# Five small constants move to the far end of SBUF, so that pools begin at multiples of 512 bytes

## The chip, the core and the metric

The kernel runs on one core of a Trainium2 chip. The core has a matrix engine (PE, with its weight loads shown apart as PEld), a vector engine (DVE), a scalar engine (ACT), GpSimd (POOL) and a sync engine (SP) that here only issues transfers. Operands live in SBUF, 128 partitions of on-chip memory; an address in this document is a byte offset within a partition, the same in all 128. Matmul results go to PSUM. The metric is the device time of one execution in microseconds, as the median of several runs. Lower is better.

## The reference

The reference is one layer of a hybrid decoder block on a sequence of 1024 tokens of width 1024, followed by a final RMS norm.

```python
mod = jax.nn.silu(c) @ ada_w + ada_b
shift, scale, gate = jnp.split(mod, 3, axis=-1)
h = rms_norm(x, norm_w) * (1 + scale[:, None, :]) + shift[:, None, :]
proj = h @ w_in
gm_u, gm_v, gm_z, ssm_z, xbc, dt_raw, g_a, g_b = jnp.split(proj, SPLITS, axis=-1)
y_a = spatial_gating(gelu(gm_u), gelu(gm_v), ...) * silu(gm_z)
xbc = silu(causal_depthwise_conv(xbc, conv_w, conv_b))
y_b = ssd_scan(xh, dt, a, bmat, cmat) + xh * d_skip[:, None]
y_b = rms_norm(y_b * silu(ssm_z), ssm_norm_w)          # per group
merged = sigmoid(g_a) * (y_a @ w_proj_a) + sigmoid(g_b) * (y_b @ w_proj_b)
x = x + gate[:, None, :] * (merged @ w_out)
out = rms_norm(x, final_norm_w)
```

By far the largest product is `h @ w_in` (1024 x 1024 by 1024 x 11296). The other large ones are `y_a @ w_proj_a`, `y_b @ w_proj_b` (inner width 2048) and `merged @ w_out`.

## The kernel before

All matrices are fp32. A large product is done in three passes of a one-pass fp32 format ("fp32r"): each operand is split into a high part and a low remainder, and high x high, high x low and low x high are accumulated. So most matmuls have the same shape: a stationary block of 128 x 128 and a moving block of 128 x 512, both fp32r, that is 512 bytes and 2048 bytes per partition. `w_in`, `w_proj_b` and `w_out` also go through a Strassen-like scheme with seven products named p1 to p7, whose sums DVE forms.

The stages in order of time:

- **Stage 1.** The input is loaded, normalised and transposed; the rows of h are made (`rows_of_h`) and split into 56 tiles of 2048 bytes in `hpool`. The first columns of the projection are multiplied beside this (`first_products`, through the helper `mm`, line 76, with stationary pieces `w0h` and `w0l` from the pool `p0`).
- **The pair stage.** `pair` works through the column blocks of `w_in`, two at a time; `product` issues its matmuls in line 560. The moving operands are the split tiles in `hpool`, the stationary operands are split weights in `wpool`. This takes more than half of the kernel. Results go through DVE and ACT into `wide` tiles in `w4pool`.
- **The SSD stage.** The scan over chunks, in fp32, with `y_a @ w_proj_a` (`proj_a`, tile `pma`, line 76) drawn in between to keep PE busy. All operands of `proj_a` are in `hpool`. The scan's tiles are in `p2r`, `p2q` and `p2x`.
- **The product with `w_proj_b`.** `multiply`, line 1459: seven products of 8 units, each unit 12 matmuls. The moving operands (`p1bh`, `p1bl` and so on) are in `hpool`; the stationary operands (`p1a` and so on, from the helper `big`) are in `p2r` and `p2q`.
- **The product with `w_out`.** `out_products`, line 1658. Its operands come from whatever has room: `hpool`, `p2r`, `p2q`.
- **The end.** The last norm factors and the stores.

The order on PE is written out by hand and pinned. DVE and ACT are ordered by a planner. Transfers are issued from SP and ACT; a buffer that is used again makes its next load wait for the last reader.

SBUF is given out by pools from both ends. A pool on the left starts where the pool below it ended; a pool on the right ends where the one above it began. Pools that are closed give their bytes to later pools, and a tile then waits for the last users of every tile whose bytes it overlaps. A tile starts at a multiple of 32 bytes. The first pool, `const`, begins at byte 16512; the usable memory ends at byte 229344. This gives the following starts before the change, worked out by the allocator from the sizes:

| pool | side | starts at | start modulo 512 | holds |
|---|---|---|---|---|
| const | left | 16512 | 128 | identity, masks, parameters |
| hpool | left | 24448 | 384 | split rows of h, later ring buffers and operands |
| p0 | left | 139136 | 384 | stage 1 |
| wpool, wspool | left | 139136, 171904 | 384, 384 | weights of the pair stage |
| w4pool | right | 204768 | 480 | `wide` tiles |
| gmpool, gxpool | right | 198624, 192832 | 480, 320 | mixer |
| prepool | right | 189408 | 480 | preparation of `w_proj_b` |
| p2r | right | 188384 | 480 | SSD, weights of line 1459 and 1658 |
| p2x, p2q | right | 172000, 139232 | 480, 480 | SSD, later operands |

Nearly every large tile is a multiple of 512 bytes long, so it has its pool's start modulo 512. The stationary operands of stage 1 are windows into tiles of 1152 bytes and start at 0, 128, 256 or 384 modulo 512.

The helpers that record most matmuls and transfers:

```python
def mm(acc, l, r, first=True, last=True):
    pin(PE.matmul(acc, l, r, start=first, stop=last))
...
def load(dst, src):
    pin(nc.sync.dma_start(dst, src))
```

The rest that the change touches is the block of constants near the start of the kernel. Of these, `sc` is read by the modulation and the gate of stage 1, `dtb` and `abc` by the step sizes (`dt_part1a`, `dt_part1d`), `dsk` and `dskt` by `small_parameters` and by `evacuate` (a per-partition factor).

Of the kernel before, what the change touches and what calls it, by code (L numbers as in the profile page):

```python
# [8 lines left out]
F32 = mybir.dt.float32  # L9
# [7 lines left out]
P = 128  # L17
D = 1024
S = 1024
KT = D // P  # L20
NCH = S // P
NG = 8
HPG = 4
NH = 32
# [11 lines left out]
def hybrid_kernel(  # L36
# [33 lines left out]
    def cst(shape, name, dt=F32):  # L70
        return const.tile(shape, dt, name=name, tag=name)

    pin = tc.keep_in_program_order

    def mm(acc, l, r, first=True, last=True):
# [33 lines left out]
    par = cst([P, P], "par")  # L109
    par2 = cst([P, P], "par2")  # L110
    cwt = cst([P, P], "cwt")
    dtb = cst([P, NH], "dtb")
    abc = cst([P, NH], "abc")
    dskt = cst([P, 16], "dskt")
    dsk = cst([P, NH], "dsk")
    sc = cst([P, KT], "sc")
    dthq = cst([P, NCH * NH], "dthq")
    dde = cst([P, NCH * NH], "dde")
    nacs = cst([P, NCH * NH], "nacs")
    cd = cst([P, NCH * NH], "cd")  # L120
    ssq = cst([P, NG * NCH], "ssq")
    conv_wt = cwt.rearrange("p (k i) -> p k i", k=4)
    conv_bt = par2[:, 0:32]
    snw = par2[:, 32:48]
# [1670 lines left out]
```

## Time and profile before

| | |
|---|---|
| median of 3 runs | 1415.43 us (1413.42 to 1416.88) |
| span of the profiled execution, first to last instruction | 1412.0 us |
| PE busy | 1386.7 us, 98% of the span, 7051 matmuls |
| PE weight loads | 1147.0 us, 81% |
| DVE, ACT, POOL busy | 1062.5, 796.2, 212.5 us |
| DMA | 283.13 MB, 201 GB/s over the span |
| mean granted PE clock | 0.998 |

The profile is one execution. No other time is listed for it than its span; the median of the runs is 3.4 us above that, which is start and end work outside the span. A row of the timeline gives start, length, engine, line, operation, tiles, shapes and count. The length of a matmul's record is longer than its share of PE, because matmuls overlap: the pace of PE is the distance from one start to the next. In the table of windows each row has the stretch, its length, then for each engine the busy time and the count, the granted clock, the DMA share and GB/s.

### The profile page before, as it was taken

What the parts mean: (1) busy time and instruction counts of PE and PEld (TensorE: products, weight loads), DVE (VectorE), ACT (ScalarE), POOL (GpSimd) and SP (SyncE); (2) the same over time, 40 slices, a digit from 0 to 9 for tenths busy, and PEclk for the clock granted to TensorE, in tenths of its full rate; (3) what the DMA queues carried; (4) which work ended last, traced back from release to release, by engine and by line L of the source; (5) the groups of instructions that cost most, each with busy time, mean ns of one, the idle gap of its engine ahead of it and who ended that gap; (6) DMA issues with size and microseconds to landing.
All of it is one profiled execution on the core that took longest, in us unless ns stands there. A gap on an engine that the chain in (4) does not pass through costs nothing. (4 is left out here: it accounts for less than half of the span.)

```text
span 1412.0 us, 20661 instructions
## 1 busy us (share of the span) xinstructions
PE 1386.7 (98%) x7051; PEld 1147.0 (81%) x7051; DVE 1062.5 (75%) x1863; ACT 796.2 (56%) x1471; POOL 212.5 (15%) x208
## 2 busy tenths in 40 slices
PE   8999999999999999999999999999999999999997
PEld 7788888888888888887888888888888878777886
DVE  5686677767778899788888785388777767866866
ACT  6664575656656665555666555586766723322443
POOL 0000000000000011110100010027878830000001
PEclk9999999999999999999999999999999999999999
DMA  8552333343344667777675774498878759867903
GB/s 269 159 166 83 127 104 108 102 128 110 121 135 127 199 197 236 244 239 233 203 205 175 243 213 134 167 347 313 279 268 286 275 188 347 307 219 267 374 6 120
DMA packets 271918, 283.13 MB, mean 201 GB/s; under 512 B 14300, under 2 KB 222596, under 8 KB 271812
## 3 DMA queue, kind: packets, MB, share of 16 engines
q1 hardware_dynamic: 184548, 198.39, 44.0%
q10 hardware_dynamic: 87264, 83.41, 17.7%
q8 instruction: 56, 0.92, 0.3%
q14 instruction: 50, 0.41, 0.1%
HBM read 194.42 MB, written 87.33 MB: 200 GB/s over the span
## 5 line engine op out<-in xcount | busy, mean ns | idle before, releaser
L775 POOL TENSOR_TENSOR wog<-wog,gb 128x256 f32<-128x256 f32 x16 | 17.0, 1080 | 673.5 <-DMA wog<-in_w_out_dram 673.5
L989 ACT ACTIVATE dcy<-dcy,nacs 128x128 f32<-128x128 f32 x256 | 78.6, 389 | 15.2 <-POOL dcy L984 14.8
L984 POOL TENSOR_SCALAR_AFFINE_SELECT dcy<-dcy 128x1024 f32<-128x1024 f32 x32 | 35.0, 1094 | 138.2 <-ACT ea L981 134.6
L902 ACT ACTIVATE ac<-ac 128x1024 f32<-128x1024 f32 x32 | 33.9, 1060 | 25.9 <-DVE ac L900 25.8
L981 ACT ACTIVATE ea<-dcy 64x512 f32<-64x512 f32 x64 | 40.1, 626 | 14.7 <-DMA dcy<-acs_d 14.2
L76 PE MATMUL pma<-yh,wah 128*128 128x512 f32 x128 | 43.3, 419 | 0.0
L76 PE MATMUL pma<-yh,wal 128*128 128x512 f32 x128 | 42.6, 414 | 0.0
L1071 POOL TENSOR_TENSOR yz<-y,sl 128x512 f32<-128x512 f32 x32 | 41.5, 1296 | 1.1
L1009 DVE TENSOR_TENSOR dcy<-dcy,pc 128x1024 f32<-128x1024 f32 x32 | 38.9, 1216 | 2.9 <-PE pc L79 1.4
L1069 DVE TENSOR_TENSOR ym<-yn,ea 128x512 f32<-128x512 f32 (+1 forms) x32 | 19.9, 622 | 27.3 <-PE yn L76 27.3
L76 PE MATMUL pma<-yl,wah 128*128 128x512 f32 x128 | 40.2, 395 | 0.0
L1070 POOL TENSOR_TENSOR y<-y,ym 128x512 f32<-128x512 f32 (+1 forms) x32 | 36.6, 1143 | 12.0 <-DVE ym L1069 11.2
L76 PEld LDWEIGHTS yn<-sl,st 128*128 128x128 f32 x224 | 30.3, 190 | 7.0 <-POOL yz L1091 2.1
L76 PE MATMUL sp<-xe,bn 128*128 128x256 f32 x112 | 32.6, 408 | 3.2 <-DVE xe L1005 1.2
L900 DVE SCALAR_TENSOR_TENSOR ac<-c2x,cwt,ac 128x1023 f32<-128x1023 f32 (+2 forms) x24 | 31.2, 1299 | 5.8 <-ACT ac L898 5.7
L1398 DVE SCALAR_TENSOR_TENSOR yn<-yn,par,rb 128x512 f32<-128x512 f32 x32 | 23.9, 748 | 15.0 <-DMA yn<-yb_d 14.6
L76 PE MATMUL yi<-dcy,xd 128*64 128x128 f32 x512 | 35.0, 279 | 0.0
L76 PE MATMUL yn<-sl,st 128*128 128x128 f32 x224 | 31.3, 276 | 3.6 <-DVE st L1039 3.6
L900 DVE SCALAR_TENSOR_TENSOR ac<-c2cb,cwt,ac 128x1023 f32<-128x1023 f32 (+2 forms) x24 | 31.2, 1299 | 4.4 <-ACT ac L898 4.3
L1673 POOL TENSOR_TENSOR r<-r,fnw 128x512 f32<-128x512 f32 x2 | 2.6, 1300 | 209.3 <-DMA out_dram<-r 209.3
L1037 POOL TENSOR_TENSOR st<-st,cd 128x256 f32<-128x256 f32 x48 | 32.5, 678 | 8.2 <-PE yn L76 5.1
L900 DVE SCALAR_TENSOR_TENSOR ac<-c1cb,cwt,ac 128x1023 f32<-128x1023 f32 (+2 forms) x24 | 31.1, 1296 | 1.4 <-ACT ac L898 1.4
(2977 smaller groups left out, 4404.0 us busy)
## 6 DMA issues: line engine op xcount, KB each, us to landing
sl<-s_d SPq DMA_DIRECT2D x32, 768.0 KB, 4.7
s_d<-ac ACTq DMA_DIRECT2D x32, 512.0 KB, 4.2
dcy<-acs_d SPq DMA_DIRECT2D x32, 512.0 KB, 9.0
aw<-in_ada_w_dram SPq DMA_DIRECT2D x16, 512.0 KB, 3.7
wbr<-in_w_proj_b_dram SPq DMA_DIRECT2D x64, 128.0 KB, 4.4
wb_d<-wbb ACTq DMA_DIRECT2D x32, 256.0 KB, 4.9
wb_d<-wbc ACTq DMA_DIRECT2D x32, 256.0 KB, 4.1
yb_d<-yz ACTq DMA_DIRECT2D x32, 256.0 KB, 5.3
```

The source lines that it names most:

```text
L76: pin(PE.matmul(acc, l, r, start=first, stop=last))
L900: V.scalar_tensor_tensor(ac[:, s:], cc[:, : S - s], conv_wt[:, 3 - s, i : i + 1], ac[:, s:], op0=ALU.mult, op1=ALU.add)
L902: A.activation(ac, ac, AF.Silu)
L981: A.activation(ea[hh * HD : (hh + 1) * HD], dcy.rearrange("p (j e) i l -> p e j (i l)", e=2)[hh * HD : (hh + 1) * HD, hh], AF.Exp)
L984: G.affine_select(out=d8, in_=d8, compare_op=ALU.is_ge, fill=-1e30, base=0, pattern=[[0, 2 * HPG], [1, P]], channel_multiplier=-1)
L989: A.activation(dcy[:, h, i, :], dcy[:, h, i, :], AF.Exp, bias=sub[:, i, h : h + 1])
L1009: V.tensor_tensor(d3, d3, pc[:, 0:256].unsqueeze(1).to_broadcast([P, HPG, 256]), op=ALU.mult)
L1037: G.tensor_mul(v3(s2), v3(self.st), fac(cd, g, s)[:, i].unsqueeze(2).to_broadcast([P, HPG, HD]))
L1069: V.tensor_tensor(m[:, :, t0:], yn.rearrange("p (j l) -> p j l", j=2)[:, :, t0:], ea[:, :, t0:], op=ALU.mult)
L1070: G.tensor_add(y1[:, :, t0:], y1[:, :, t0:], m[:, :, t0:])
L1071: G.tensor_mul(yz, y1, sl[:, 4:6])
L1398: V.scalar_tensor_tensor(t, t, snw[:, n : n + 1], rbs[n // 2, h], op0=ALU.mult, op1=ALU.mult)
```

## The change

Five constants (`dtb`, `abc`, `dskt`, `dsk`, `sc`; 128, 128, 64, 128 and 32 bytes per partition, 480 in all) leave `const` and go into a new pool `edge`, which is the first pool on the right and so takes the last 480 bytes. `ssq` becomes 24 columns (96 bytes) longer; the added columns are never read or written. The `const` pool so shrinks by 384 bytes. Every left pool after it begins 384 bytes lower, every right pool 480 bytes lower.

```diff
+    edge = ctx.enter_context(tc.tile_pool(name="edge", bufs=1, side="right"))
+
+    def edg(shape, name):
+        return edge.tile(shape, F32, name=name, tag=name)
+
...
-    dtb = cst([P, NH], "dtb")
-    abc = cst([P, NH], "abc")
-    dskt = cst([P, 16], "dskt")
-    dsk = cst([P, NH], "dsk")
-    sc = cst([P, KT], "sc")
+    dtb = edg([P, NH], "dtb")
+    abc = edg([P, NH], "abc")
+    dskt = edg([P, 16], "dskt")
+    dsk = edg([P, NH], "dsk")
+    sc = edg([P, KT], "sc")
...
-    ssq = cst([P, NG * NCH], "ssq")
+    ssq = cst([P, NG * NCH + 24], "ssq")
```

By subtraction `hpool` then begins at 24064, `wpool` and `p0` at 138752, `wspool` at 171520, `w4pool` at 204288, `prepool` at 188928, `p2r` at 187904, `p2x` at 171520 and `p2q` at 138752: all multiples of 512. `const` itself still begins at 16512. `gxpool` ends at a multiple of 512 and begins at 192352, which is none; no fp32r operand lies in it. Before, `p2x` and `p2q` lay 96 bytes higher than `wspool` and `wpool`, whose bytes they take over; after, they lie exactly on them.

## The prediction

> **What bounds the kernel now.** I read the page first, then the busy times by stage, then the chain that ended last, and then the timeline of PE in four places. The busy times by stage, whose columns are PE, PEld, DVE, ACT and POOL, then granted clock, DMA share and GB/s:
>
> ```profile
> 0.00:50.00 50.00, 45.32 (x324) 36.80 (x325) 27.41 (x66) 32.15 (x55) 3.15 (x10) 1.00 0.83 251
> 50.00:100.00 50.00, 50.00 (x274) 39.10 (x274) 38.09 (x70) 32.23 (x56) 0.00 (x0) 1.00 0.48 139
> 150.00:900.00 750.00, 748.68 (x3380) 620.13 (x3379) 592.30 (x998) 441.90 (x720) 29.56 (x24) 1.00 0.56 171
> 900.00:1000.00 100.00, 98.75 (x639) 83.64 (x639) 69.96 (x120) 76.34 (x182) 49.02 (x50) 1.00 0.85 293
> 1000.00:1100.00 100.00, 95.58 (x743) 83.70 (x742) 75.67 (x139) 69.34 (x182) 81.30 (x78) 1.00 0.81 280
> 1200.00:1300.00 100.00, 97.86 (x415) 77.53 (x414) 68.93 (x110) 28.32 (x47) 0.00 (x0) 1.00 0.78 269
> 1300.00:1412.00 112.00, 102.90 (x453) 83.15 (x452) 85.67 (x155) 44.57 (x92) 6.03 (x7) 0.97 0.45 168
> ```
>
> PE sets the time. From 150 to 900 us it idles for 1.3 us in all. So an edit that leaves the work as it is can gain in two ways: by the few idle spots of PE, or by the pace at which PE takes its matmuls. The chain that ended last (start, length, what) gives that pace for the last two products:
>
> ```profile
> 1186.47 30.94 PE yp L1459 x132
> 1217.41 0.02 issue
> ...
> 1219.29 7.68 DMA yn<-yb_d
> ...
> 1257.12 42.18 PE x L1459 x180
> 1299.30 0.02 issue
> 1299.31 3.28 DMA p4a<-wb_d
> ...
> 1325.00 11.09 PE ox L1658 x48
> 1336.09 11.15 PE oy L1658 x48
> 1347.24 33.43 PE ox L1658 x144
> 1380.67 19.53 PE oy L1658 x84
> ```
>
> In line 1459 this is 42.18 / 180 = 234.3 ns a matmul. In line 1658 it is (11.09 + 11.15 + 33.43 + 19.53) / 324 = 75.20 / 324 = 232.1 ns. These matmuls have the same form as those of the pair stage (line 560) and of `proj_a` (line 76, tile `pma`): stationary 128 x 128, moving 128 x 512, fp32r. The timeline of PE shows the pace there:
>
> ```profile
> 305.22 1.07 PE L560 MATMUL xx<-t4h,p4x1h 128*128 128x512 f32 x4
> 306.13 1.07 PE L560 MATMUL xx<-t4l,p4x1h 128*128 128x512 f32 x4
> 307.04 1.07 PE L560 MATMUL xx<-t4h,p4x1l 128*128 128x512 f32 x4
> 307.94 1.07 PE L560 MATMUL xuz<-t2h,p6uz3h 128*128 128x512 f32 x4
> ```
>
> ```profile
> 1152.17 0.70 PE L76 MATMUL pma<-yh,wah 128*128 128x512 f32 x2
> ...
> 1154.57 0.62 PE L76 MATMUL pma<-yh,wal 128*128 128x512 f32 x2
> 1155.02 0.62 PE L76 MATMUL pma<-yh,wah 128*128 128x512 f32 x2
> ...
> 1158.65 0.62 PE L76 MATMUL pma<-yh,wal 128*128 128x512 f32 x2
> 1159.10 0.39 PE L1459 MATMUL x<-p1bh,p1a 128*128 128x512 f32 x1
> ```
>
> Line 560 takes (307.94 - 305.22) / 12 = 226.7 ns. Line 76 takes (1159.10 - 1154.57) / 20 = 226.5 ns, right before line 1459 begins its 234 ns. The granted clock is 1.00 in all these stages.
>
> What differs? In line 560 and in `proj_a` the moving and the stationary operand both begin at 384 modulo 512. In line 1459 the moving operand is in `hpool` (384) and the stationary one in `p2r` or `p2q` (480). In line 1658 there are all mixtures. The stage is not the cause: `proj_a`, like line 1459, uses each stationary block for two matmuls running and changes the PSUM bank often, and DMA is as busy around it. Nor is the region: `p2q` and `wpool` cover the same bytes but for 96. The start of the operand is left, and the change moves just that.
>
> **The change, part by part.**
>
> *No instruction is added or removed.* The new pool holds the same five tiles, and the 24 columns of `ssq` aren't touched. I take 0 for this.
>
> *Where transfers may start.* `p2q` and `p2x` now lie exactly on the tiles of `wpool` and `wspool`, so a new tile there overlaps one old tile fewer and its load waits for fewer readers. Such loads are at the start of the SSD stage, and PE idles 1.25 us from 900 to 1000 us. The gain is between 0 and 1.25 us. I take 0, since PE waits there for DVE (`yn` and `sp` wait for `st` and `xe`), as the waits of PE show:
>
> ```profile
> PE yn L76 <- DVE st L1039: 3.6, 4, 1.9
> PE pp L79 <- DMA pk<-in_ada_b_dram: 3.5, 1, 3.5
> PE yp L1459 <- DVE c L1612: 1.3, 3, 0.8
> PE sp L76 <- DVE xe L1005: 1.2, 2, 0.6
> ```
>
> *DVE and ACT.* The same DVE subtraction takes as long with all operands at 384 (first row) as with all at 480 (second):
>
> ```profile
> L1431 DVE TENSOR_TENSOR yn<-yn,yn 128x512 f32<-128x512 f32 x8 | 5.5, 685 | 0.1
> L1443 DVE TENSOR_TENSOR p2a<-p2r,p2a 128x512 fp32r<-128x512 f32 x8 | 5.5, 686 | 0.3 <-ACT p2a L1442 0.3
> ```
>
> So I take 0 for the engines other than PE.
>
> *Line 1459.* Both operands will begin at 0 modulo 512. No row shows fp32r pairs at 0/0 in a steady run, so the pace must be bounded. The nearest rows are 384/384, also equal and also a multiple of 128: 226.7 ns. The other end is the first stretch of line 1658, whose moving operands are two thirds at 480 and whose stationary ones are all at 480: 11.09 / 48 = 231.0 ns. I take 226.7, because 384 shares with 0 that it is a multiple of 128; 480 isn't even one of 64. The counts come from the busy times of these two lines:
>
> ```profile
> 0.00:1412.00 1412.00, 159.86 (x672) 125.84 (x672) 1.00 0.62 201
> 1325.00:1400.00 75.00, 75.00 (x324) 60.68 (x324) 1.00 0.32 120
> ```
>
> 672 x (234.3 - 226.7) = 5.1 us. Some of it is lost. `p3` waits for DVE, which waits for the transfer `yn<-yb_d`, which PE released at 1217.4 us. What PE gains before that moves the transfer too; what the rest of `p2` gains (about 58 matmuls, 0.4 us) turns into waiting. The same holds after `p4a<-wb_d` at 1299.3 us (0.2 us). That leaves 4.5 us. The operands are otherwise there in time: DVE is busy for 69% of that stage.
>
> *Line 1658.* 324 x (232.1 - 226.7) = 1.8 us. It's all on the path, since PE is busy for the whole stretch.
>
> *Line 560 and `proj_a`.* Both operands go from 384 to 0 together. I take 0, as they pace at 226.7 already; the bounds are in the rivals. The fp32 matmuls of the scan I leave as they are.
>
> The sum is -6.3 us. The profiled span is 1412.0 us and becomes 1405.7. The median lies 3.4 us above that span; the forecast for the median is 1409.1 us (-0.45%).
>
> [...]
>
> **The rivals.**
>
> *No effect (1415.4 us).* The pace of 234 ns comes from the order in which line 1459 takes its operands (moving high, low, high; a new PSUM bank after every third matmul), not from where they begin. For it: DVE shows nothing of the start. Against it: `proj_a` has as many repetitions and bank changes and still settles at 226.5 ns, and line 1658 keeps its 232 ns with twelve matmuls to a bank.
>
> *Slower.* What counts is the offset itself, and 0 is as bad as 480. Then pairs at 0/0 pace at 231.0 ns. From that pace on, it is line 560 that decides, with 43 column pairs x 7 products x 12 = 3612 matmuls by the code: with the 528 fp32r matmuls of line 76 (384 of `proj_a`, 144 of stage 1) it would lose 4140 x 4.3 = 17.8 us, while lines 1459 and 1658 win 672 x 3.3 + 324 x 1.1 = 2.6 us. That gives 1430.6 us. The break-even is near 228 ns. Against it: in stage 1 the stationary pieces begin at 0, 128, 256 and 384 in turn, and 50 to 100 us shows PE as full as ever; but no run there is long enough to settle.
>
> *Faster everywhere.* A start at a multiple of 256 or 512 saves as much again over 384 as 384 does over 480, 7.6 ns. Over 3612 + 528 + 672 + 324 = 5136 matmuls that is another 39 us: about 1370 us. Nothing in the profile asks for it; nothing excludes it. [...]
>
> *Faster transfers alone.* If transfers run quicker from rounder addresses and PE keeps its pace, the gain is bounded by PE's idle spots that a transfer ends: 4.7 us in the first 50 us (3.5 of it for `pk`, a first small load that alignment can hardly help) and about 1 us through `yn` in line 1459. I take 2 us: 1413.4 us. [...]
>
> **How the numbers follow.** The forecast has 0.60, of which 0.03 lands within 0.3% because only part of the pace comes; no effect 0.20 (0.02 of it slower, through a planner that orders DVE or ACT a little differently); slower through 0/0 0.12; faster everywhere 0.05; faster transfers alone 0.03 (0.02 of it faster than 0.3%). About 0.3%, 4.2 us, is what a measurement of this kernel can tell from no change. Faster: 0.57 + 0.05 + 0.02 = 0.64. Same: 0.03 + 0.18 + 0.01 = 0.22. Slower: 0.02 + 0.12 = 0.14. The likeliest case alone has 1406 to 1412 us. For 8 in 10 the range reaches over the case of no effect and the spread of the runs, 1404 to 1417.5 us; it leaves out the slower rival and the one that is faster everywhere.
>
> **What would show it.** In the timeline after, line 1459 and line 1658 should step by 226 to 227 ns as line 560 does, with the chain's `L1459 x180` or its like at 40.8 us in place of 42.2. Line 560 should keep 226.7 ns and `proj_a` 226.5. DVE's 685 ns and ACT's lengths should stay. The forecast is wrong if line 1459 still paces at 234 ns (then order, not address), if line 560 moves at all (then the offset itself counts, by 3.6 us for each ns), or if PE gets new waits for DVE after 1150 us, where line 1459 would then be fed too slowly.

## The result and the profile after

| | before | changed |
|---|---|---|
| median | 1417.13 us (1413.42 to 1422.91, 11 runs) | 1412.33 us (1408.00 to 1414.36, 11 runs) |
| ratio to before, as recorded | 1 | 0.9954, 95% interval 0.9938 to 0.9970 |
| span of the profiled execution | 1412.0 us | 1411.7 us |

The changed kernel is faster by 0.46%. The recorded ratio isn't the quotient of the two medians, which is 0.9966: the 11 runs of the kernel before include the three that had been measured before the prediction, and these were quick. The other eight have a median of 1418.83 us, and 1412.33 / 1418.83 = 0.9954. The two profiled spans don't show it, for a reason that the second profile of the kernel before gives below. The program has the same instructions in the same order on each engine; line numbers are 5 higher (`mm` L81, `product` L565, `multiply` L1464, `out_products` L1663).

The busy times by stage of the changed kernel (PE, PEld, DVE, ACT, POOL, then clock, DMA share, GB/s):

```profile
0.00:50.00 50.00, 45.05 (x324) 35.92 (x325) 27.27 (x66) 32.19 (x55) 3.14 (x10) 1.00 0.79 252
150.00:900.00 750.00, 746.61 (x3372) 618.50 (x3371) 590.85 (x994) 441.43 (x718) 32.70 (x24) 1.00 0.55 170
900.00:1000.00 100.00, 99.32 (x640) 84.13 (x639) 71.95 (x123) 76.03 (x180) 47.66 (x48) 1.00 0.85 297
1000.00:1100.00 100.00, 93.57 (x727) 81.93 (x727) 72.52 (x132) 68.70 (x182) 79.83 (x78) 1.00 0.80 273
1200.00:1300.00 100.00, 97.44 (x426) 79.29 (x425) 72.60 (x116) 30.29 (x50) 0.00 (x0) 1.00 0.80 278
```

PE is as full as before. From 1200 to 1300 us it gets through 426 matmuls in place of 415, in slightly less busy time. Its chain that ended last (start, length, what):

```profile
1191.57 29.93 PE yp L1464 x132
...
1223.38 7.63 DMA yn<-yb_d
...
1260.51 40.93 PE x L1464 x180
1301.44 0.02 issue
1301.46 3.11 DMA p4a<-wb_d
...
1326.50 10.88 PE ox L1663 x48
1337.38 10.88 PE oy L1663 x48
1348.26 32.64 PE ox L1663 x144
1380.90 19.04 PE oy L1663 x84
```

Line 1464 takes 29.93 / 132 = 226.7 ns a matmul, where the 132 before took 30.94 us (234.4 ns). The four pieces of line 1663 take 73.44 / 324 = 226.7 ns. The timeline of PE in the pair stage and in the last of `proj_a`:

```profile
305.45 1.07 PE L565 MATMUL xx<-t4h,p4x1h 128*128 128x512 f32 x4
306.36 1.07 PE L565 MATMUL xx<-t4l,p4x1h 128*128 128x512 f32 x4
307.26 1.07 PE L565 MATMUL xx<-t4h,p4x1l 128*128 128x512 f32 x4
308.17 1.07 PE L565 MATMUL xuz<-t2h,p6uz3h 128*128 128x512 f32 x4
...
1158.62 0.62 PE L81 MATMUL pma<-yh,wal 128*128 128x512 f32 x2
...
1163.15 0.39 PE L1464 MATMUL x<-p1bh,p1a 128*128 128x512 f32 x1
```

Line 565 steps by (308.17 - 305.45) / 12 = 226.7 ns as before, and `proj_a` by (1163.15 - 1158.62) / 20 = 226.5 ns. The busy time of PE in one line alone, over the whole execution, is the steadiest measure of pace, since idle time doesn't enter it. For the changed kernel, lines 565, 1464 and 1663:

```profile
0.00:1500.00 1500.00, 828.72 (x3612) 675.74 (x3612) 1.00 0.58 189
0.00:1500.00 1500.00, 155.22 (x672) 125.28 (x672) 1.00 0.58 189
0.00:1500.00 1500.00, 76.47 (x348) 63.82 (x348) 1.00 0.58 189
```

and for the kernel before, lines 560 and 1658 (line 1459 stands in the prediction with 159.86 us):

```profile
0.00:1500.00 1500.00, 828.61 (x3612) 675.70 (x3612) 1.00 0.58 189
0.00:1500.00 1500.00, 78.21 (x348) 63.83 (x348) 1.00 0.58 189
```

So PE has 4.64 us less work in the product with `w_proj_b`, 1.74 us less in the product with `w_out`, and none less in the pair stage: 6.4 us. The weight loads (second column) are as long as before to 0.6 us, 125.28 against 125.84 us in the product with `w_proj_b`; it is the spacing of the matmuls that shrank.

Not all of it reaches the end. From the first matmul of line 1464 to the first of line 1663 (1163.15 to 1326.34 us) the stage takes 163.2 us; before it took 165.7 us (1159.10 to 1324.84). That is 2.5 us less with 4.64 us less work, so PE idles 2.1 us more. Its waits (in total, times, longest):

```profile
PE yn L81 <- DVE st L1044: 4.6, 5, 2.2
...
PE xz L565 <- DVE c2z L581: 1.9, 2, 1.7
PE xg L565 <- DVE c2g L581: 1.5, 1, 1.5
...
PE yp L1464 <- DVE c L1617: 1.3, 3, 0.8
PE yp L1464 <- ACT p3bh L1442: 1.3, 1, 1.3
...
PE x L1464 <- DVE tha L1295: 1.2, 1, 1.2
...
PE yp L84 <- POOL ssq L1108: 1.0, 1, 1.0
```

In the first profile of the kernel before, whose rows for these were shorter:

```profile
PE xz L560 <- DVE c2z L576: 0.8, 1, 0.8
...
PE xg L560 <- DVE c2g L576: 0.5, 2, 0.3
...
PE yp L1459 <- ACT p3bh L1437: 0.9, 1, 0.9
...
PE x L1459 <- DVE tha L1290: 0.4, 1, 0.4
...
PE yp L79 <- POOL ssq L1103: 0.2, 1, 0.2
```

the waits for `p3bh`, `tha` and `ssq`, all in the stage of line 1459, come to 1.5 us; after they come to 3.5 us. These 2.0 us are nearly all of the 2.1. I read it so: a faster PE arrives earlier at operands that DVE, ACT and POOL make at their old pace. One pair of profiles doesn't show it, since these waits also differ between executions of one kernel (1.9 us in the second profile of the kernel before). The same DVE subtraction as in the prediction, at its new addresses:

```profile
L1448 DVE TENSOR_TENSOR p2a<-p2r,p2a 128x512 fp32r<-128x512 f32 x8 | 5.5, 685 | 1.2 <-ACT p2a L1447 1.2
L1436 DVE TENSOR_TENSOR yn<-yn,yn 128x512 f32<-128x512 f32 x8 | 5.5, 684 | 0.1
```

### The profile page after: what moved, and what is told of

It reads as the page before. It is cut to its first block, busy times and chain, and to the rows that moved or that the text cites. A ratio compares the mean times of both kernels' runs of the same rounds, so it can differ in the third digit from the quotient of the medians.

```text
span 1411.7 us, 20659 instructions
## 1 busy us (share of the span) xinstructions
PE 1380.4 (98%) x7051; PEld 1145.7 (81%) x7051; DVE 1063.0 (75%) x1863; ACT 796.2 (56%) x1471; POOL 215.7 (15%) x208
## 5 line engine op out<-in xcount | busy, mean ns | idle before, releaser
L780 POOL TENSOR_TENSOR wog<-wog,gb 128x256 f32<-128x256 f32 x16 | 20.3, 1290 | 676.4 <-DMA wog<-in_w_out_dram 644.4
L81 PE MATMUL pma<-yh,wah 128*128 128x512 f32 x128 | 43.4, 420 | 0.0
L81 PE MATMUL pma<-yh,wal 128*128 128x512 f32 x128 | 42.5, 413 | 0.0
L81 PE MATMUL pma<-yl,wah 128*128 128x512 f32 x128 | 40.1, 395 | 0.0
L81 PEld LDWEIGHTS yn<-sl,st 128*128 128x128 f32 x224 | 30.3, 190 | 8.1 <-POOL yz L1096 2.3
L81 PE MATMUL sp<-xe,bn 128*128 128x256 f32 x112 | 32.6, 408 | 4.2 <-DVE ym L1074 1.3
L81 PE MATMUL yn<-sl,st 128*128 128x128 f32 x224 | 31.6, 276 | 4.6 <-DVE st L1044 4.6
L81 PE MATMUL yi<-dcy,xd 128*64 128x128 f32 x512 | 35.0, 279 | 0.2 <-DVE st L1044 0.2
```

## The experiments

The prediction came out, but it had chosen 226.7 ns for starts at 0/0 on a guess: that a start is good when it is a multiple of 128 (384 and 0 are, 480 isn't). Other rules fit the two traces as well. Three were set against each other:

- A: what counts is each operand's own start, and multiples of 64 or 128 are good.
- B: what counts is that moving and stationary operand start at the same offset.
- C: what counts is a start at a multiple of 256 or 512.

From here on a pair such as 384/480 is the start modulo 512 of left pools (moving) and right pools (stationary of line 1459), and "difference" is stationary minus moving.

### The changed kernel again, and the same start elsewhere

The changed kernel a second time:

> The changed kernel once more, beside the next three on one chip. Lines 1464 and 1663 at 226.7 ns a matmul as in its first profile; time 0.994 to 0.997 of before. If the gain came from the pace alone, the stages up to line 1464 take as long as before (within the spread of executions), and lines 1464 and 1663 together are 4 to 6.5 us shorter.

The kernel before with both ends at 384. An unused tile of 96 bytes takes the end of the right side; the constants stay where they were:

```diff
+    edge = ctx.enter_context(tc.tile_pool(name="edge", bufs=1, side="right"))
...
+    edg([P, 24], "pad")
```

> The kernel before, with 96 bytes of padding ahead of the right pools and nothing moved: left pools at 384 modulo 512, right pools at 384 too, none at 0. Theory A (a start at a multiple of 64 or 128 bytes is what counts): line 1459 at 226.7 ns, time as the changed kernel, 0.994 to 0.997. Theory B (moving and stationary operand must have the same offset): the same. Theory C (a start at 0 modulo 256 or 512 is needed): line 1459 stays at 231 to 235 ns, time 1.000.

Both ends at 480. This is one line of the change alone:

```diff
-    ssq = cst([P, NG * NCH], "ssq")
+    ssq = cst([P, NG * NCH + 24], "ssq")
```

> The kernel before, with ssq 96 bytes longer and nothing moved: left pools at 480 modulo 512 as the right ones are. The right pools then lie exactly on the left ones they take over, as in the changed kernel. Theory A: line 560 and all else pace at 231 to 235 ns instead of 226.7, 3612 x 4.3 to 8 = 15 to 30 us slower, 1.01 to 1.02. Theory B: 226.7 ns everywhere, 0.994 to 0.997. A theory by which the exact overlay of the pools brings the gain: 0.995 with 234 ns in line 1459.

Both ends at 448, a multiple of 64 but not of 128:

```diff
+    edg([P, 8], "pad")
...
-    ssq = cst([P, NG * NCH], "ssq")
+    ssq = cst([P, NG * NCH + 16], "ssq")
```

> The kernel before with 64 bytes more in ssq and 32 bytes of padding on the right: all pools at 448 modulo 512, a multiple of 64 and not of 128. Theory A with 64: 226.7 ns everywhere, 0.994 to 0.997. Theory A with 128: as at 480/480, 231 to 235 ns in line 560, 1.01 to 1.02. Theory B: 0.994 to 0.997.

All four ran beside the kernel before (1419.17 us, 20 runs). The ratios are the recorded ones and differ a little from the quotients of the medians. The last three columns are PE's busy us in the lines of `product`, `multiply` and `out_products`, for the kernel before from its first profile.

| starts | median us | ratio, 95% interval | L560 | L1459 | L1658 |
|---|---|---|---|---|---|
| 384/480 (before) | 1419.17 | 1 | 828.61 | 159.86 | 78.21 |
| 0/0 again | 1413.20 | 0.9958 (0.9944 to 0.9972) | 829.43 | 156.32 | 76.47 |
| 384/384 | 1412.58 | 0.9959 (0.9945 to 0.9974) | 828.50 | 155.24 | 76.47 |
| 480/480 | 1412.94 | 0.9956 (0.9939 to 0.9973) | 828.88 | 155.19 | 76.47 |
| 448/448 | 1414.52 | 0.9965 (0.9952 to 0.9978) | 829.08 | 155.28 | 76.47 |

The chain of the kernel with 480/480:

```profile
1186.99 29.93 PE yp L1459 x132
...
1255.68 40.88 PE x L1459 x180
...
1321.62 10.88 PE ox L1658 x48
1332.50 10.88 PE oy L1658 x48
```

480/480 is as fast as 0/0. A falls with 480/480 and C with 384/384; B stands. The second run of 0/0 has 1.1 us more busy time in this line, though its piece of 132 matmuls takes 29.93 us there too. Its trace shows a slow stretch: where `p3` begins, the granted clock is 0.54 from 1238 to 1240 us, and PE is busy for 1.69 us there with 4 matmuls, where 4 of line 565 running take 1.07 us. The row of this stretch, clock third from the end:

```profile
1238.00:1240.00 2.00, 1.69 (x4) 0.86 (x5) 2.00 (x4) 0.00 (x0) 0.00 (x0) 0.54 0.42 171
```

With 480/480 the same line of code, with the same order of operands, takes 226.7 ns, and 234 ns before, so the order isn't the cause either.

### The other part alone

The changed kernel without the 24 columns: the five constants move, the starts become 416/0. Both are new, and the difference is 96 bytes again (0 - 416 modulo 512).

> The changed kernel without the 24 columns of ssq: the five constants move to the right, and the left pools begin at 416, the right ones at 0 modulo 512. Both starts are new, the difference between the operands of line 1459 is 96 bytes again. If the difference sets the pace: line 1459 at 234 ns, line 1658 near 232, line 560 at 226.7, time as before, ratio 1.000 within 0.002. If a start at 0 on the right is what helps: line 1459 near 227, ratio 0.996. If a left start of 416 hurts: line 560 above 226.7 ns, by 3.6 us for each ns.

It took 1422.36 us beside 1418.97 us of the kernel before: recorded ratio 1.0016, 0.9993 to 1.0039. Its chain:

```profile
1196.50 30.94 PE yp L1464 x132
...
1268.45 42.18 PE x L1464 x180
```

These are the two lengths of the kernel before to the hundredth. Line 1663 steps by 232.3 ns, as line 1658 does before, and line 565 is busy for 830.47 us. So the move of the constants, taken alone, brings no gain; the part of the change that no instruction ever touches, 96 unused bytes, brings all of it when it is made alone.

### The slow pace moved into the pair stage

If the difference is the cause, line 560 must be slowed by it too. A gap of 96 bytes at the end of `hpool` puts `wpool` at 480, while its moving operands stay at 384:

```diff
     bop[nm] = [[hp.tile([P, 512], F32R, ...
+    hp.tile([P, 24], F32, name="gap", tag="gap")
```

> A gap of 96 bytes at the end of hpool moves wpool, wspool and p0 to 480 modulo 512, with the right side. The moving operands stay at 384. So line 560 (line 561 here) gets the pair of starts, 384 moving and 480 stationary, that line 1459 had before, and line 1459 keeps it. If the difference between the two starts sets the pace: line 560 goes from 226.7 to about 234 ns, 3612 x 7.6 = 27 us, the time becomes about 1444 us (ratio 1.019), line 1459 stays at 234 ns and proj_a, both operands in hpool, at 226.5 ns. If the slow pace belongs to line 1459's own order or to bytes in p2r and p2q: line 560 stays at 226.7 ns and the time at about 1417 us.

The time rose to 1439.64 us beside 1417.86: recorded ratio 1.0164, 1.0142 to 1.0185 (the quotient of the medians is 1.0154). PE's busy time in the pair stage's line, over the whole execution, two rows of its timeline, 36 matmuls apart, and a piece of line 1460, which is line 1459 before:

```profile
0.00:1500.00 1500.00, 853.91 (x3612) 678.44 (x3612) 1.00 0.59 189
```

```profile
310.23 1.10 PE L561 MATMUL yuz<-t1l,p5uz3h 128*128 128x512 f32 x4
...
318.66 1.10 PE L561 MATMUL yuz<-b22l,p3uz3h 128*128 128x512 f32 x4
```

```profile
1211.79 30.94 PE yp L1460 x132
```

8.43 / 36 = 234.2 ns: the pair stage has taken on the pace that line 1459 had, and that line keeps it. `proj_a`, both of whose operands are in `hpool`, takes 4.58 us for a piece of 20 matmuls in the chain, as it does with 448/448. The busy time rose by 25.3 us, the kernel by 23.3 us (0.0164 of 1417.86; 20.1 to 26.2). That is the cause shown on the other product, with unchanged instructions and nearly unchanged weight loads (678.4 against 675.7 us). The 27 us expected was too high: 25.3 us are 7.0 ns for each of the 3612 matmuls and not 7.6. The gain in line 1464 falls short in the same way (4.64 us / 672 = 6.9 ns). Why is left open.

This kernel also answers the theory that it is the exact overlay of the pools that helps. In every kernel with equal starts `p2q` begins on the byte where `wpool` began. Here it does too (139232), and line 1460 is slow all the same. In the kernel with starts 0, 128 and 256 in the next part it doesn't (139008 on 138880), and its line 1464 is fast.

### How the pace depends on the difference

Four kernels have `hpool` at 0 and set `wpool` and the right side by gaps; `dskt` and `sc` are back in `const`, and `abc`, `dtb` and `dsk` share bytes with `cd`, `dde` and `nacs`. Only the sizes differ; the remarks at the ends of the lines, which aren't in the code, give those of all four:

```diff
+    edg([P, 104], "pad")                        # right 64;  256: 56;  192: 72;  384: 24 columns
...
+    hp.tile([P, 8], F32, name="gap", tag="gap") # wpool 32;  128: 32;  160: 40;  256: 64 columns
```

> Equal kernel but for where pools begin: hpool 0, wpool 32, right side 64 modulo 512; dtb, abc and dsk share the bytes of cd, dde and nacs. Line 560 so has a difference of 32 bytes between stationary and moving operand, line 1459 one of 64. If any difference is as bad as 96: both lines at 231 to 235 ns, and the time about 1417 + 3612 x 7.6 ns = 1444 us. If the cost grows with the difference: line 560 between 227 and 234 ns, about 229, and 1425 us. If only differences that are no multiple of 64 cost: line 560 at 234, line 1459 at 226.7 ns.

> As the one before with hpool 0, wpool 128, right side 256 modulo 512: line 560 has a difference of 128 bytes, line 1459 one of 256. If only equal starts modulo 512 are fast: both at 231 to 235 ns, the time about 1444 us. If differences that are multiples of 128 cost nothing: both at 226.7 ns, about 1412 us. If some difference is better than none: below 226.7 ns in one of the two.

> As the one before with hpool 0, wpool 256, right side 384 modulo 512: line 560 has a difference of 256 bytes, line 1459 one of 384. If only equal starts modulo 512 are fast: both at 231 to 235 ns, the time about 1444 us. If differences that are multiples of 128 cost nothing: both at 226.7 ns, about 1412 us. If 256 is special (half a stationary row): line 560 differs from line 1459.

> hpool 0, wpool 160, right side 192 modulo 512; otherwise as the run with 32 and 64. Line 560 has a difference of 160 bytes, line 1459 one of 192. If the pace depends on the difference modulo 256 and only 0 is free: both at 231 to 235 ns, time about 1438 us. If the cost falls off towards 256, line 1459 (192) is quicker than line 560 (160).

Here the timeline of line 565 in the kernel with 128 and 256, rows 36 matmuls apart, and a piece of its chain:

```profile
310.49 1.10 PE L565 MATMUL xx<-t4h,p4x1h 128*128 128x512 f32 x4
...
318.87 1.08 PE L565 MATMUL zuz<-b21h,p2uz3h 128*128 128x512 f32 x4
```

```profile
1208.84 29.93 PE yp L1464 x132
```

8.38 / 36 = 232.8 ns at a difference of 128, and 29.93 / 132 = 226.7 ns at 256. The same two readings of the kernel with 256 and 384:

```profile
310.12 1.07 PE L565 MATMUL xuz<-t2h,p6uz3l 128*128 128x512 f32 x4
...
318.28 1.07 PE L565 MATMUL xuz<-t3h,p7uz3l 128*128 128x512 f32 x4
```

```profile
1190.89 30.69 PE yp L1464 x132
```

8.16 / 36 = 226.7 ns at 256, and 30.69 / 132 = 232.5 ns at 384. With the other two kernels, read in the same way:

| difference, bytes | 0 | 32 | 64 | 96 | 128 | 160 | 192 | 256 | 384 |
|---|---|---|---|---|---|---|---|---|---|
| ns a matmul | 226.7 | 233.3 | 233.4 | 234.2 to 234.4 | 232.8 | 233.6 | 229.0 | 226.7 | 232.5 |

Both lines agree at 96 and at 256, so it isn't a property of one line. The fast differences are 0 and 256. 128 and 384, which are the same modulo 256, are both slow. All differences tried fit a rule modulo 256, as long as all pairs of a line have the same difference. (Line 1658, where they are mixed, is taken up below.) The theory that the cost grows with the difference falls with 32 bytes, which cost nearly as much as 96. The times follow: 1438.11 us (32 in the pair stage), 1431.27 us (128), 1434.88 us (160), and 1417.07 us (256), one execution each, beside 1417.86 us of the kernel before in three of them and 1418.97 us for 160. The kernel with 256 and 384 has the paces of the kernel before: the pair stage, at 256, as fast as with equal starts, and line 1464, at 384, slow. No difference gave a pace below 226.7 ns.

### The kernel before, profiled a second time

> The kernel before, profiled a second time, to see how much the stages scatter from one execution to the next. If the address sets the pace: line 1459 at 234 ns and line 1658 at 232 ns again. The pair stage and the SSD stage should differ from the first profile by up to some us, as those of the changed kernels did; if they come out as in the first profile (851.1 us from the first to the last start in line 560), the changed kernels really lose 1 to 2 us there.

This execution took 1420.79 us, its span 1419.1 us, 7.1 us more than the first profile's. Its chain:

```profile
1193.38 30.94 PE yp L1459 x132
...
1264.08 42.19 PE x L1459 x180
...
1331.99 11.15 PE ox L1658 x48
```

The pace of line 1459 is that of the first profile; the first stretch of line 1658 takes 11.15 us here where it took 11.09. By the starts in the two timelines, the 7.1 us are 1.7 us before line 560, 0.5 us within the pair stage, 4.4 us from the last matmul of line 560 to the first of line 1459 and 0.45 us in line 1459. One wait of the SSD stage that the first profile doesn't have at all stands out among the waits of PE:

```profile
PE yn L76 <- POOL yz L1091: 2.7, 1, 2.7
```

So executions of one kernel differ by several us in the SSD stage, and the first profile was a quick one. In the profiles of the five runs with equal starts that stage took between 1.3 us less and 5.8 us more than in the first profile. What makes it scatter wasn't looked into.

The pair stage is less clear. From the first to the last start of line 560 the kernel before takes 851.1 and 851.6 us in its two profiles; the five runs with equal starts take 851.3 to 853.3 us, with the same busy time to 1 us. In the changed kernel's first profile the waits for `c2z` and `c2g`, shown above, are 2.1 us longer than in that of the kernel before. Up to 2 us may so be lost in this stage through the new addresses; two profiles on one side don't settle it.

## Why the prediction was right, and where it wasn't

The forecast was 1409.1 us, a ratio of 0.9955 to 1415.43; measured were 1412.33 us and 0.9954. The time is 3.2 us above the forecast, because the kernel before was slower in the runs beside it: 1418.83 us in the median of eight, 3.4 us above 1415.43. The mechanism, a faster pace of PE in lines 1459 and 1658 and nowhere else, was right; the reason for expecting it was not. That the ratios agree to 0.0001 is luck: the interval reaches from 4 to 9 us of gain, and in the one pair of profiles the stages of the two products became 4.3 us shorter, not 6.3.

**No instruction, DVE, ACT.** Taken at 0, and so it is: 684 and 685 ns against 685 and 686. This DVE subtraction takes 684 to 686 ns at starts of 0, 384 and 480, while fp32r matmuls take 226.7 or 234.2 ns for the same instructions, with every start a multiple of 32 bytes.

**Transfers.** Taken at 0. The stretch from 900 to 1000 us has 0.7 us of idle PE in place of 1.25, less than the scatter just shown. No effect can be told, for or against.

**Line 1459, the pace.** 226.7 ns was right and worth 4.64 us of busy time, where the prediction had 5.1. The reason given for taking it was wrong: "384 shares with 0 that it is a multiple of 128; 480 isn't even one of 64". With 480/480 the pace is 226.7 ns as well, and with 0/128, two multiples of 128, it is 232.8. What 384/384 and 0/0 share is that the two operands start alike. So the right pace was chosen by luck, for a reason that doesn't hold. I had noted that line 560 has both operands at one offset and line 1459 has not, and then read the offset where the difference was the finding. The other end of the bounds, 231.0 ns, had the same fault: in that stretch of line 1658 a third of the moving operands stood at a difference of 96, and with all operands at 480 the same 48 matmuls take 10.88 us, 226.7 ns each. The 5.1 us were also too much because 672 matmuls were counted at the 7.6 ns of a long piece; on average each gave 6.9 ns.

**Line 1459, what is lost.** The 0.6 us taken for this was too small in this profile: 2.1 us were lost, nearly all in the waits for `p3bh`, `tha` and `ssq`. The sentence that the operands are "otherwise there in time", drawn from DVE's 69%, failed: an average says nothing about the single hand-over. The amount varies: in the kernel with 480/480 the stage took 161.75 us (1159.70 to 1321.45), 4.0 us less than before, and there the loss was 0.7 us, about as forecast.

**Line 1658.** -1.8 us forecast, -1.74 us of busy time measured, and the same in every kernel with equal starts.

**Line 560 and `proj_a`.** Line 560 is busy for 828.61 and 828.72 us, `proj_a` steps by 226.5 ns both times: no change, as forecast. This was luck of a kind, since the reason given was their pace before, and what it took was that their two operands keep equal starts; a gap of 96 bytes at that place costs 23 us.

**From the span to the median.** "3.4 us above that span, which is start and end work outside the span" was wrong. In every run that has both, the device time is 1.7 to 1.9 us above its span (1413.41 and 1411.7 for the changed kernel). The other 1.7 us were that the profile shows an execution quicker than the median. This is also why the spans, 1412.0 and 1411.7 us, hide the gain: the first is of a quick run of its kernel, the second of an ordinary one.

**The rivals.** *No effect* fell with 480/480, where the order of the operands is the old one and the pace is not. *Slower* rested on 480 being bad in itself; it isn't (226.7 ns with 480/480). A slower kernel was to be had (1439.64 us with the gap of 96 bytes), but by a difference between the two ends, not by a start. *Faster everywhere* would need a pace under 226.7 ns; among nine differences none gave it. *Faster transfers alone*: PE's busy time in the two lines fell by 6.4 us and its idle time didn't, while this rival had PE keep its pace and wait less.

## What to carry to other kernels

When two matmul stages of the same shape pace differently, compare the addresses of the two operands with each other, and not each with a round number: here streams of fp32r matmuls, 128x128 by 128x512, are 1.0 to 3.4% slower at the seven differences tried that aren't 0 modulo 256. Pools that grow from both ends of the memory get out of step through any odd size among small constants, and one padded tile sets that right. One moving operand in three at another offset is enough for more than half of the full loss (the first stretch of line 1658 before: 231.0 ns, between 226.7 and 234.3). To see a gain of a few us, compare the busy time of the affected line and repeat the profile of the kernel before, since spans of single executions scatter by more (1412.0 and 1419.1 us for the kernel before).

## What the hardware showed unexpectedly

The pace of PE depended on the distance of two operands in memory, by 2 to 8 ns of 227, though the weight loads hardly changed in length (188 ns each for `p2a`, before and after). The records of the matmuls got shorter by about as much as their spacing, from 396 to 389 ns for `p2bh,p2a`. Not every distance costs the same: 192 bytes cost 2.3 ns a matmul and 64 bytes 6.7 ns, though they differ from a multiple of 256 by as much; 192 and 160 were each seen in one kernel only. The cost isn't simply paid by each pair for itself. In line 1658 of the kernel before, by the addresses that its tiles are given, 200 of the 324 matmuls of 512 columns have equal starts and 124 don't. If each paid for its own pair, the mean would be (200 x 226.7 + 124 x 234.3) / 324 = 229.6 ns; it is 232.1. From start to start in the first profile, those with equal starts take 231.9 ns on average and the others 232.5: a matmul with equal starts is slowed too when it stands among others. Which pair of operands has to be alike (those of one matmul, the stationary block of a matmul and the moving operand of the one ahead of it, or the moving operands of two matmuls in a row), and what makes a difference cost time, no run here shows.

Plain fp32 matmuls didn't show the effect where it could be read: the records of 128x128 ones, of which `mix` has 128 for its 64 matmuls, step by 111 to 112 ns in the kernel before, both in the scan's `pc<-sl`, where the difference is 0, and in the mixer's `mix`, where it is 160 modulo 256 (worked out from their starts).
